# A two-layer decoder trunk on one core: modulation weights transposed in DRAM and summed along the free axis, weight units stored as SBUF holds them

## The chip, the cores and the metric

The kernel runs on one core of a Trainium2 chip. The metric is the time of one execution on the device in microseconds (us); lower is better. The engines that matter here are TensorE (PE, with its weight loads as PEld), VectorE (DVE), ScalarE (ACT), GpSimd (POOL) and SyncE (SP), whose queue issues nearly all transfers from DRAM. They run side by side, each working through its own instructions in order, and they wait for one another through semaphores.

## The reference, cut to what matters

One sequence of 256 tokens with 2048 features passes through two layers. Layer 0 mixes by causal pooling, layer 1 by multi-head latent attention; each has a SwiGLU feed-forward part (FFN) with 5632 inner features. Every sub-layer gets a shift, a scale and a gate, which are vectors of 2048 numbers computed from one conditioning vector `c`:

```python
sc = jax.nn.silu(c)                                   # (1, 2048)
for i in range(2):
    shift_m, scale_m, gate_m, shift_f, scale_f, gate_f = split(sc @ mod_w[i] + mod_b[i], 6)
    if i == 1:
        kv_shift, kv_scale = split(sc @ kv_mod_w + kv_mod_b, 2)
        h_kv = rmsnorm(x, kv_in_norm) * (1 + kv_scale) + kv_shift
        kv = shared_kv(h_kv, ...)
    h = rmsnorm(x, norm_mix[i]) * (1 + scale_m) + shift_m
    x = x + gate_m * (pool_mixer(h) if i == 0 else mla_mixer(h, kv))
    h = rmsnorm(x, norm_ffn[i]) * (1 + scale_f) + shift_f
    x = x + gate_f * ((silu(h @ ffn_gate[i]) * (h @ ffn_up[i])) @ ffn_down[i])
return rmsnorm(x, final_norm)
```

`mod_w[i]` has 2048 rows and 6 x 2048 columns. Each of these products is one row times a large matrix: 14 vectors of 2048 results from 16 MB of weights each (12 from `mod_w`, 2 from `kv_mod_w`), all float32.

## The kernel before, in words

**Weight units.** The large products run on TensorE. A weight unit is a block of 512 rows and 512 columns (1 MB). `w_unit` loads it into a slot of the ring "raw" (six slots of 8 KB per partition), ScalarE writes its upper half (L440), VectorE the rest (L442), both into the ring "hl", and TensorE multiplies with three combinations of halves: 24 matmuls of 512 columns per unit (L464). In DRAM the weights lie as in the reference, so a partition of a unit is four pieces of 2 KB.

**The opening.** The first four modulation products (shift, scale and gate of the pooling mixer, and the first 512 columns of the FFN's shift and scale) are needed at once. `Strips` computes them on TensorE with 32-column weights (L274), 16 units of 1 MB for each of the first three (rows of 8 KB), and 8 units for the last, each loaded as two transfers of 512 KB whose rows are pieces of 2 KB. Some of the gate's units are summed on VectorE instead (L257, L259). The order of work in this stage is written out by hand.

**The background.** All other modulation products run on VectorE beside the matmuls. `Part` handles one vector of 2048 results: for each of 16 row blocks of the weight (128 x 2048) one instruction adds weight times `s_col` (silu of `c`, one number per partition) to an accumulator of 128 x 2048 (L230). `BlockPart` handles 512 columns of shift and of scale together: 8 units, each loaded as two transfers and added with two instructions of 128 x 1024 (L305). The accumulator then holds 128 partial sums per column. `folded` sums them: per 512 columns one 32 x 32 block transpose (L320) and one reduction (L321) on VectorE, then a matmul with a 0/1 matrix (L326), and four small VectorE instructions on 32 partitions each, which write the columns (L343, L346, L357, L935, L936). The bias comes in by loading it into row 0 of the accumulator, which POOL sets to zero first (L220, L298).

**Pace.** `background` is a list of these units. Each weight unit calls `tick`, which issues background units at a planned rate (`plan`, `release`); `flush` runs what stands in `pending` after a given number of weight units, placed behind that unit's two halves. `folded` puts its pieces there while `pieced` is true; during the attention stage it issues them at once. The scheduler of the framework orders the rest by priority; the stretches between an FFN and what follows are in a written order.

**End of an FFN.** `FFN_STEPS` gives the order of a layer's FFN: p for a chunk of gate and up projection, t for its transposition, d for a group of the down projection. The last are "p10 t9 t10 d3". `StreamEnd` adds the gated result to the stream. Its method `known` does what doesn't need the last group: for 512 columns and both token tiles it multiplies the sum so far by the gate (L673) and adds the stream (L674). In d3 it is called for the first columns at the start and for the next columns at each step.

**Vectors.** Norm gains, `c` and the biases of the opening are loaded as rows by eight small transfers and turned on TensorE (L192, L200, L205).

Of the kernel before, what the change touches and what calls it, by code (L numbers as in the profile page):

```python
# [17 lines left out]
P = 128  # L18
# [31 lines left out]
C_FOLD = C_SIGN + 1  # L50
C_SEL = C_FOLD + P
# [14 lines left out]


LATE, MLA_LATE, WO_LATE = 3, 5, 3

FOLD_WAIT = 2  # L70

V_NM, V_NF, V_KVIN, V_KVN, V_QN, V_PS, V_END = 0, 32, 64, 80, 84, 88, 104


def shape_constants():
    con = np.zeros((P, C_END), np.float32)
    con[:, C_ID:C_ID + P] = np.eye(P, dtype=np.float32)
    q = np.arange(P)
    con[:, C_MASK:C_MASK + P] = np.where(q[None, :] <= q[:, None], 0.0, NEG)
    freq = (10000.0 ** (-np.arange(0, ROPE, 2, dtype=np.float64) / ROPE)).astype(np.float32)  # L80
    con[:, C_FREQ] = freq[q % HALF]
    con[:, C_FOLD:C_FOLD + P] = q[:, None] % 32 == q[None, :] % 32
# [13 lines left out]
def tile_trunk(ctx: ExitStack, tc: tile.TileContext, a: dict, out: bass.AP):  # L96
# [41 lines left out]
    fold = con[:, C_FOLD:C_FOLD + P]  # L138
    crow = t2k([KD, P])
    vrows = t2k([V_END, P])  # L140
    brows = t2k([5 * KD, P])
# [3 lines left out]

    def load_rows(first, name, pattern, **sizes):
        src = a[name].rearrange(pattern, q=P)
        sync.dma_start(vrows[first:first + src.shape[0]], src)
# [13 lines left out]
    load_rows(V_NM, "norm_mix", "l (r q) -> (l r) q")  # L162
    load_ahead()
    load_rows(V_NF, "norm_ffn", "l (r q) -> (l r) q")
    load_rows(V_KVIN, "kv_in_norm", "(r q) -> r q")
    load_x(1)
    load_rows(V_KVN, "kv_norm", "(r q) -> r q")
    load_ahead()
    load_rows(V_QN, "q_norm", "l (r q) -> (l r) q")
    load_rows(V_PS, "pool_scale", "l (r q) -> (l r) q")  # L170
    load_ahead()
    sync.dma_start(brows, a["mod_b"][0, :5 * D].rearrange("(r q) -> r q", q=P))
# [10 lines left out]
    front = work.tile([P, KD * (STRIP + 7) + STRIP], F32, tag="acc", bufs=2, name="front")  # L183
    s_strip = front[:, :KD * STRIP].rearrange("p (k m) -> p k m", m=STRIP)
    one_strip = front[:, KD * (STRIP + 7):]
    bcol = front[:, KD * STRIP:KD * (STRIP + 5)].rearrange("p (i k) -> p i k", k=KD)
    gm_col, ps_col = (front[:, KD * (STRIP + i):KD * (STRIP + i + 1)] for i in (5, 6))
    pool.memset(front[:, :KD * STRIP], 0.0)
    pool.memset(one_strip, 0.0)
    pool.memset(one_strip[:, 0:1], 1.0)  # L190
    cps = ps_t()
    pe.transpose(cps[:, :KD], crow, ident[:KD, :KD])  # L192
    s_col = const.tile([P, KD], F32, name="s_col")
    act.activation(s_col, cps[:, :KD], AF.Silu)
    dve.tensor_copy(s_strip[:, :, 0], s_col)
    vcol = const.tile([P, V_PS], F32, name="vcol")

    def vectors():
        vps = ps_t()
        pe.transpose(vps[:, :V_END], vrows, ident[:V_END, :V_END])  # L200
        dve.tensor_copy(vcol, vps[:, :V_PS])
        dve.tensor_copy(ps_col, vps[:, V_PS:V_END])

        bps = ps_t()
        pe.transpose(bps[:, :5 * KD], brows, ident[:5 * KD, :5 * KD])  # L205
        for i in range(5):
            dve.tensor_scalar(out=bcol[:, i], in0=bps[:, i * KD:(i + 1) * KD], scalar1=1.0 if i in (1, 4) else 0.0,
                              scalar2=None, op0=ALU.add)
# [4 lines left out]
    class Part:  # L213
        def __init__(self, w, b, done):
            self.w, self.b, self.done, self.kt = w, b, done, 0

        def unit(self):
            if self.kt == 0:
                self.acc = work.tile([P, D], F32, tag="acc", bufs=2, name=nm("acc"))
                pool.memset(self.acc, 0.0)  # L220
                sync.dma_start(self.acc[0:1, :], self.b)
            r = raw_t([P, D])
            sync.dma_start(r, self.w[self.kt * P:(self.kt + 1) * P, :])
            self.add(r)
            self.kt += 1
            if self.kt == KD:
                self.done(self.acc)

        def add(self, r):
            dve.scalar_tensor_tensor(out=self.acc, in0=r, scalar=s_col[:, self.kt:self.kt + 1],  # L230
                                     in1=self.acc, op0=ALU.mult, op1=ALU.add)
# [3 lines left out]
    class Strips:  # L235
        def __init__(self, i, pair, done, aside=()):
            self.aside, self.acc, self.bank = aside, None, None
            self.n, self.rows, self.done, self.kt = (2, 2, done, 0) if pair else (NSTRIP, 1, done, 0)
            w = a["mod_w"][0][:, i * D:(i + self.rows) * D]
            self.w = w.rearrange("(k p) (i n) -> p k i n", p=P, i=2)[:, :, :, :CH] if pair else                 w.rearrange("(k p) (i n) -> p k i n", p=P, i=NSTRIP)  # L240
# [10 lines left out]
        def use(self, r):  # L251
            last = self.kt + self.rows == KD
            if self.kt in self.aside:
                s_ = s_col[:, self.kt:self.kt + 1]
                if self.acc is None:
                    self.acc = work.tile([P, 1, NSTRIP, CH], F32, tag="acc", bufs=2, name=nm("acc"))
# [31 lines left out]


    class BlockPart:  # L290
        def __init__(self, w, b, col, done):
            self.w, self.b, self.col, self.done, self.kt = w, b, col, done, 0

        def unit(self):
            pick = slice(self.col, self.col + CH)
            if self.kt == 0:
                self.acc = work.tile([P, 2, CH], F32, tag="acc", bufs=2, name=nm("acc"))
                pool.memset(self.acc, 0.0)  # L298
                sync.dma_start(self.acc[0:1], self.b.rearrange("o (i n) -> o i n", i=2)[:, :, pick])
            r = raw_t([P, 2, 2, CH])  # L300
            rows = self.w[self.kt * P:(self.kt + 2) * P, :].rearrange("(k p) (i n) -> p k i n", p=P, i=2)
            for k in range(2):
                sync.dma_start(r[:, k], rows[:, k, :, pick])
            for k in range(2):
                dve.scalar_tensor_tensor(out=self.acc, in0=r[:, k], scalar=s_col[:, self.kt + k:self.kt + k + 1],  # L305
                                         in1=self.acc, op0=ALU.mult, op1=ALU.add)
            self.kt += 2
            if self.kt == KD:
                self.done(self.acc)

    pending, pieced = [], [True]

    def folded(acc, n, fin):


        part = acc[:, :n // 32]

        def piece(i):
            tr, ns = t2k([P, CH]), slice(i * CH, (i + 1) * CH)
            dve.transpose(tr, acc[:, ns])  # L320
            dve.tensor_reduce(out=part[:, i * (CH // 32):(i + 1) * (CH // 32)], in_=tr.rearrange("p (b j) -> p b j", j=32),  # L321
                              axis=AX.X, op=ALU.add)

        def finish():
            pt = ps_t()
            pe.matmul(pt[:, :n // 32], lhsT=fold, rhs=part, start=True, stop=True)  # L326
            v = pt[:, :n // 32].rearrange("p (k r) -> p k r", r=4)
            for r in range(4):
                rows = slice(32 * r, 32 * r + 32)
                fin(v[rows, :, r], rows)  # L330
        n_ = n // CH
        for i in range(n_):
            if pieced[0]:
                pending.append((i // 2 if n_ == 2 else i, lambda i=i: piece(i)))
            else:
                piece(i)
        pending.append((n_ + 1 if pieced[0] and n_ > 2 else FOLD_WAIT, finish))

    def to_cols_folded(fin):
        return lambda acc: folded(acc, D, fin)  # L340

    def shift_to(i):
        return to_cols_folded(lambda pt, rows: dve.tensor_copy(cols[rows, i, :], pt))  # L343

    def scale_to(i, g):
        return to_cols_folded(lambda pt, rows: dve.scalar_tensor_tensor(  # L346
            out=cols[rows, i, :], in0=pt, scalar=1.0, in1=vcol[rows, g:g + KD], op0=ALU.add, op1=ALU.mult))
# [3 lines left out]
    def gate_to(name):  # L351
# [3 lines left out]

        def fin(pt, rows):
            dve.tensor_copy(col[rows], pt)  # L357
            if rows.stop == P:
                pending.append((0, spread))
# [9 lines left out]
        return to_cols_folded(fin)  # L369

    def mod_part(l, i, done):
        cs = slice(i * D, (i + 1) * D)
        return Part(a["mod_w"][l][:, cs], a["mod_b"][l:l + 1, cs], done)

    def kv_part(i, done):
        cs = slice(i * D, (i + 1) * D)
        return Part(a["kv_mod_w"][:, cs], a["kv_mod_b"][None, cs], done)
# [70 lines left out]
    def w_unit(src):  # L448
        if repr(src) in early:
            return early.pop(repr(src))  # L450
        shape = [P, KL, src.shape[1]]
        r = raw_t(shape)
        w_load[0] = sync.dma_start(r, src.rearrange("(k p) n -> p k n", p=P))
# [23 lines left out]
    def proj(src, tiles):  # L477
        banks = [ps_t() for _ in range(NT)]
        for u in range(len(tiles)):
            hi, lo = w_unit(src[u * CH:(u + 1) * CH, :])  # L480
# [1152 lines left out]
```

## Time and profile before

| | |
|---|---|
| median of 3 runs | 1937.2 us (1936.84 to 1937.63) |
| the profiled execution | 1935.94 us, span of the trace 1934.2 us |
| TensorE granted clock, mean | 0.983 |
| busy: PE, DVE, ACT, POOL | 97%, 77%, 44%, 3% |
| moved by DMA | 575.08 MB, mean 297 GB/s |

All rows below are from that one execution. "Busy" is the time in which an engine had an instruction under way; for TensorE it includes the overlap of pipelined matmuls, so 100% busy isn't yet full speed. A row of waits names the engine and line that sat idle, what released it, and the total, the number and the longest of these waits. A row of windows gives for a stretch of the span each engine's busy time and instruction count, the granted TensorE clock, the busy share of the DMA engines and their rate. A row of groups gives a line's engine, operation, tiles, shapes and count, then total busy time and mean ns of one, then the idle time just before them.

### The profile page before, as it was taken

The numbers are of one execution on the slowest core, as the hardware profiler recorded it, in microseconds if no ns is written. First come the engines' busy times: TensorE is split into PE (matmuls) and PEld (weight loads), VectorE is DVE, ScalarE is ACT, GpSimd is POOL, SyncE is SP. The second block draws the span as 40 slices with busy tenths as digits, with TensorE's granted clock in tenths as the row PEclk, the third lists the DMA queues.
The fourth block names the chain that finished last, engine by engine and source line by source line (L and its number), as shares of the span: only waits on it lengthen the run. The fifth ranks groups of instructions, "written<-read, shape, count | busy, mean of one in ns | idle before, by whom it ended". The sixth has DMA issues, their size and how long they took to land.

```text
span 1934.2 us, 22338 instructions
## 1 busy us (share of the span) xinstructions
PE 1866.6 (97%) x8836; PEld 1511.7 (78%) x8836; DVE 1482.1 (77%) x1419; ACT 849.2 (44%) x954; POOL 49.4 (3%) x46
## 2 busy tenths in 40 slices
PE   6689999999999999999999999999999999999998
PEld 3156887888888888787879888888888888888887
DVE  2148899999878788888799986989886565555656
ACT  3024634443433344335678735634444433333333
POOL 0000000000000000001200000000000000000000
PEclk9689999999999999999999999999999999999999
DMA  9999999889898999998698695998886667666651
GB/s 397 411 416 387 386 364 320 303 308 362 322 344 318 339 336 331 353 337 273 214 341 297 213 332 187 386 334 312 279 291 239 231 240 255 235 205 236 218 196 44
DMA packets 226114, 575.08 MB, mean 297 GB/s; under 512 B 12109, under 2 KB 16709, under 8 KB 203859
## 3 DMA queue, kind: packets, MB, share of 16 engines
q1 hardware_dynamic: 225482, 570.49, 81.5%
q0 software_dynamic: 432, 3.15, 0.4%
q8 instruction: 69, 1.13, 0.2%
q14 instruction: 35, 0.29, 0.0%
q10 hardware_dynamic: 96, 0.02, 0.0%
HBM read 567.31 MB, written 6.32 MB: 297 GB/s over the span
## 4 chain that ended last, share of the span: by engine, by line
PE 89%; DMA 5%; DVE 3%; ACT 2%; issue 1%; POOL 0%; SPq 0%; POOLq 0%; DVEq 0%; ACTq 0%
PE ps L464 77%; DMA raw<-in_mod_w_dram 4%; PE ps L473 2%; PE ps L1048 2%; PE ps L1363 2%; PE ps L274 1%; PE ps L798 1%; DVE hl L442 1%; DMA act<-in_x_dram 1%; DVE acc L230 1%; PE ps L1271 1%; DMA raw<-in_ffn_up_dram 0%; PE ps L606 0%; PE ps L1023 0%; PE ps L840 0%
## 5 line engine op out<-in xcount | busy, mean ns | idle before, releaser
L464 PE MATMUL ps<-hl,act 128*128 128x512 f32 x6744 | 1549.7, 391 | 6.9 <-DVE hl L442 4.3
L464 PEld LDWEIGHTS ps<-hl,act 128*128 128x128 f32 x6744 | 1266.2, 188 | 271.5 <-DVE hl L442 5.2
L440 ACT ACTIVATE hl<-raw 128x2048 fp32r<-128x2048 f32 x289 | 552.9, 1917 | 619.9 <-PE ps L464 505.4
L442 DVE TENSOR_TENSOR hl<-raw,hl 128x2048 fp32r<-128x2048 f32 x289 | 660.7, 2288 | 201.4 <-ACT hl L440 200.6
L230 DVE SCALAR_TENSOR_TENSOR acc<-raw,s_col,acc 128x2048 f32<-128x2048 f32 x112 | 262.8, 2346 | 0.7 <-DMA raw<-in_mod_w_dram 0.6
L305 DVE SCALAR_TENSOR_TENSOR acc<-raw,s_col,acc 128x1024 f32<-128x1024 f32 x112 | 143.4, 1280 | 2.2 <-DMA raw<-in_mod_w_dram 0.7
L274 PE MATMUL ps<-raw,front 128*32 128x512 f32 x392 | 66.6, 744 | 25.6 <-DMA raw<-in_mod_w_dram 25.5
L767 DVE TENSOR_TENSOR act<-ps,act 128x512 f32<-128x512 f32 x96 | 64.1, 684 | 10.5 <-PE ps L464 10.2
L274 PEld LDWEIGHTS ps<-raw,front 128*32 128x32 f32 x392 | 9.7, 119 | 60.9 <-DMA raw<-in_mod_w_dram 48.4
L1363 PE MATMUL ps<-act,hl 128*128 128x256 f32 x384 | 48.8, 284 | 0.0
L473 PE MATMUL ps<-hl,act 128*128 128x512 f32 x192 | 47.0, 399 | 1.2 <-DVE act L569 0.9
L1363 PEld LDWEIGHTS ps<-act,hl 128*128 128x128 f32 x384 | 47.5, 192 | 0.7 <-DVE act L1327 0.2
L801 ACT ACTIVATE act<-ps 128x512 fp32r<-128x512 f32 x44 | 23.8, 595 | 52.6 <-PE ps L798 45.0
L281 DVE COPY t2k<-ps 128x256 f32<-128x256 f32 x4 | 1.7, 424 | 57.5 <-ACT t2k L280 57.5
L856 DVE TENSOR_TENSOR x<-ps,x 128x512 f32<-128x512 f32 x32 | 22.1, 691 | 30.1 <-PE ps L464 30.1
L473 PEld LDWEIGHTS ps<-hl,act 128*128 128x128 f32 x192 | 35.1, 188 | 10.9 <-ACT act L556 1.8
L867 ACT ACTIVATE t2k<-ps 128x512 f32<-128x512 f32 x24 | 14.2, 592 | 62.6 <-PE ps L464 62.5
L493 ACT ACTIVATE junk<-x 128x512 bf16<-128x512 f32 x23 | 14.6, 633 | 60.7 <-DVE x L681 39.9
L871 DVE TENSOR_TENSOR t2k<-ps,t2k 128x512 f32<-128x512 f32 x24 | 16.5, 688 | 25.3 <-PE ps L464 25.3
L1048 PEld LDWEIGHTS ps<-act,act 128*128 128x128 f32 x128 | 24.5, 198 | 11.5 <-issue 8.4
L1048 PE MATMUL ps<-act,act 128*128 128x256 f32 x128 | 31.7, 400 | 0.0
L802 DVE TENSOR_TENSOR act<-ps,act 128x512 fp32r<-128x512 f32 x44 | 28.2, 684 | 4.3 <-ACT act L801 4.1
(233 smaller groups left out, 1001.6 us busy)
## 6 DMA issues: line engine op xcount, KB each, us to landing
raw<-in_mod_w_dram SPq DMA_DIRECT2D x128, 1024.0 KB, 6.9
raw<-in_ffn_gate_dram SPq DMA_DIRECT2D x88, 1024.0 KB, 5.7
raw<-in_ffn_up_dram SPq DMA_DIRECT2D x88, 1024.0 KB, 6.5
raw<-in_ffn_down_dram SPq DMA_DIRECT2D x88, 1024.0 KB, 5.5
raw<-in_mod_w_dram SPq DMA_DIRECT2D x128, 512.0 KB, 6.5
raw<-in_kv_mod_w_dram SPq DMA_DIRECT2D x32, 1024.0 KB, 5.9
raw<-in_w_o_dram SPq DMA_DIRECT2D x16, 1024.0 KB, 8.8
raw<-in_w_uq_dram SPq DMA_DIRECT2D x8, 768.0 KB, 5.1
```

The lines of the kernel that those rows point to most:

```text
L230: dve.scalar_tensor_tensor(out=self.acc, in0=r, scalar=s_col[:, self.kt:self.kt + 1], in1=self.acc, op0=ALU.mult, op1=ALU.add)
L274: pe.matmul(self.bank[m * STRIP:(m + 1) * STRIP, :], lhsT=weights(k), rhs=r[:, k, i, :], start=first, stop=last)
L305: dve.scalar_tensor_tensor(out=self.acc, in0=r[:, k], scalar=s_col[:, self.kt + k:self.kt + k + 1], in1=self.acc, op0=ALU.mult, op1=ALU.add)
L440: hi_ins = act.activation(hi, r, AF.Copy)
L442: lo_ins = dve.tensor_tensor(out=lo, in0=r, in1=hi.bitcast(F32), op=ALU.subtract)
L464: pe.matmul(banks[tok], lhsT=t_[:, i, k, tok * P:(tok + 1) * P], rhs=w[:, k, :], start=first and n < len(part), stop=last and n >= len(ord ...
L473: pe.matmul(bank, lhsT=t_[:, i, k, tok * P:(tok + 1) * P], rhs=w[:, k, :], start=first and n == 0, stop=last and n == len(order) - 1)
L767: dve.tensor_tensor(out=part, in0=banks[tok], in1=part, op=ALU.add)
L801: act.activation(m[:, 0, :, ts_], v, AF.Copy)
L802: dve.tensor_tensor(out=m[:, 1, :, ts_], in0=v, in1=m[:, 0, :, ts_].bitcast(F32), op=ALU.subtract)
L1048: pe.matmul(mixed[g][:, n % 2, :], lhsT=wp[g][:, k, ns], rhs=pool_all[g // 2][:, g % 2, k, :], start=k == 0, stop=k == KL - 1)
L1363: pe.matmul(pt[:, h, :], lhsT=w(h0 + h, k), rhs=t_[:, i, k, :], start=n == 0, stop=n == 3 * KL - 1)
```

## The change

- `mod_w` and `kv_mod_w` are also laid out transposed in DRAM, on the host. A background unit is now 128 results by 2048 inputs, one transfer of 1 MB whose rows are 8 KB. One VectorE instruction multiplies it with `s_row` (silu of `c`, the same on all partitions) and sums along the free axis into one column of `sums`; the product goes back into the raw tile. `BlockPart` is gone: its work is a `Part` of 8 such units.
- `folded`, its transposes, reductions and matmuls, the accumulators, their memsets and bias loads are gone. The results already are columns; one or two small VectorE instructions add bias and apply the gain.
- All weights of w_unit, and the opening's last product, are laid out so that a unit is one contiguous megabyte, 8 KB per partition.
- Vectors are stored as columns and loaded by one transfer (128 x 344) ahead of `x`. A second copy of `c`, as a row, is spread over the partitions by four matmuls with a row of ones (`silu_row`).
- `known` is cut into 8 pieces (columns by token tile) that go to `pending` at chunk p10, with the waits in `KNOWN`; the flush at the start of d3 is gone.

```diff
+KNOWN = (1, 3, 5, 7, 9, 10, 11, 12)
-FOLD_WAIT = 2
...
+    sync.dma_start(vcol, a["vectors"])
     load_x(0)
-    sync.dma_start(crow, a["c"].rearrange("b (r q) -> (b r) q", q=P))
     sync.dma_start(con, a["con"])
...
+    def silu_row():
+        act.activation(crow, crow, AF.Silu)
+        for j in range(ND):
+            js = slice(j * CH, (j + 1) * CH)
+            pt = ps_t()
+            pe.matmul(pt, lhsT=ones[0:1, :], rhs=crow[:, js], start=True, stop=True)
+            act.activation(s_row[:, js], pt, AF.Copy)
...
     class Part:
         def unit(self):
-            if self.kt == 0:
-                self.acc = work.tile([P, D], F32, tag="acc", bufs=2, name=nm("acc"))
-                pool.memset(self.acc, 0.0)
-                sync.dma_start(self.acc[0:1, :], self.b)
+            if self.n == 0:
+                self.sums = work.tile([P, KD], F32, tag="sums", bufs=3, name=nm("sums"))
             r = raw_t([P, D])
-            sync.dma_start(r, self.w[self.kt * P:(self.kt + 1) * P, :])
-            self.add(r)
-        def add(self, r):
-            dve.scalar_tensor_tensor(out=self.acc, in0=r, scalar=s_col[:, self.kt:self.kt + 1],
-                                     in1=self.acc, op0=ALU.mult, op1=ALU.add)
+            sync.dma_start(r, self.w[self.tiles[self.n] * P:(self.tiles[self.n] + 1) * P, :])
+            dve.scalar_tensor_tensor(out=r, in0=r, scalar=1.0, in1=s_row, op0=ALU.mult, op1=ALU.mult,
+                                     accum_out=self.sums[:, self.n:self.n + 1])
...
         def load(self):                      # Strips
             r = raw_t([P, self.rows, self.n, CH])
-            for k in range(self.rows):
-                sync.dma_start(r[:, k], self.w[:, self.kt + k])
+            sync.dma_start(r.rearrange("p k i n -> p (k i n)"), self.w[self.kt // self.rows])
...
-    class BlockPart:
-    def folded(acc, n, fin):
...
+    def shift_to(i, first):
+        return lambda sums: dve.tensor_tensor(out=cols[:, i, :], in0=sums, in1=bias(first, KD), op=ALU.add)
+    def scaled_sums(dst, sums, first, g):
+        dve.scalar_tensor_tensor(out=dst, in0=sums, scalar=1.0, in1=bias(first, dst.shape[1]), op0=ALU.add, op1=ALU.add)
+        dve.tensor_tensor(out=dst, in0=dst, in1=vcol[:, g:g + dst.shape[1]], op=ALU.mult)
...
     def w_unit(src):
-        w_load[0] = sync.dma_start(r, src.rearrange("(k p) n -> p k n", p=P))
+        w_load[0] = sync.dma_start(r.rearrange("p k n -> p (k n)"), src)
...
-            self.known(0)
-        def known(self, j):
+        def known(self, j, tok, gate):
...
-                flush()
                 end = stream_end[0]
                 end.start(gates[gate_name])
...
-                    if last and c == g[0]:
-                        end.known(j + 1)
...
             if c == NF - 1:
-                stream_end.append(StreamEnd(l))
+                end = StreamEnd(l)
+                stream_end.append(end)
+                for n, wait in enumerate(KNOWN):
+                    pending.append((wait, lambda n=n: end.known(n // NT, n % NT, gates[gate_name])))
...
+def units(w):
+    k, n = w.shape
+    w = w.reshape(k // CH, KL, P, n // CH, CH).transpose(0, 3, 2, 1, 4)
+    return w.reshape(k // CH, n // CH, P, KL * CH)
...
+    o["mod_wt"] = o["mod_w"].transpose(0, 2, 1)
+    o["kv_mod_wt"] = np.asarray(i["kv_mod_w"]).T
+    block = o["mod_w"][0].reshape(KD // 2, 2, P, 6, D)[:, :, :, 3:5, :CH]
+    o["mod_block"] = block.transpose(0, 2, 1, 3, 4).reshape(KD // 2, P, 4 * CH)
```

More of the change, by code (lines that the diff above doesn't have):

```diff
@@ L311, in tile_trunk @@
-    pending, pieced = [], [True]
-    def folded(acc, n, fin):
[L316 to L347, printed above, removed]
+    pending = []
+    def shift_to(i, first):
+        return lambda sums: dve.tensor_tensor(out=cols[:, i, :], in0=sums, in1=bias(first, KD), op=ALU.add)
```

213 lines of the change are left out of this document (88 added, 125 removed).

## The prediction

> **What bounds the kernel now.** I read the page first, then the chain of work that ended last, then TensorE's waits after the opening, then windows by stage.
>
> ```profile
> span 1934.2 us, 22338 instructions
> ...
> PE 1866.6 (97%) x8836; PEld 1511.7 (78%) x8836; DVE 1482.1 (77%) x1419; ACT 849.2 (44%) x954; POOL 49.4 (3%) x46
> ```
>
> TensorE is busy for 97% of the span, so what the change does to VectorE counts only where TensorE waits for it. The chain shows two parts.
>
> ```profile
> 169.52 56.22 PE ps L464 x240
> 225.88 62.49 PE ps L464 x276
> ```
>
> Until 169.5 us the opening runs; from there the chain is matmuls back to back, 62.49 / 276 = 226 ns each. How the opening is bound is seen in two windows of it (the last two columns are DMA busy share and GB/s):
>
> ```profile
> 145.00:165.00 20.00, 19.09 (x121) 9.94 (x122) 16.07 (x34) 10.64 (x18) 1.22 (x2) 1.00 1.05 387
> 20.00:140.00 120.00, 96.63 (x540) 46.24 (x536) 41.00 (x86) 21.11 (x42) 0.00 (x0) 0.82 1.02 416
> ```
>
> The DMA engines are full in both, so the opening lasts as long as its bytes. The rate differs: 416 GB/s while nearly all loads have rows of 8 KB, 387 where the last product and the first weight units come in pieces of 2 KB. For the rest, TensorE's waits from 169 us to the end:
>
> ```profile
> PE ps L464 <- DVE hl L442: 4.3, 1, 4.3
> PE ps L326 <- issue: 4.3, 1, 4.3
> PE ps L1483 <- ACT t2k L1476: 3.1, 2, 1.6
> PE ps L464 <- DVE cols L936: 1.2, 2, 0.8
> ...
> PE ps L326 <- DVE act L767: 0.5, 1, 0.5
> ...
> PE ps L464 <- DVE act L767: 0.3, 1, 0.3
> ```
>
> These are 13.7 us of waits in 1764.7 us. So the ceiling is low whatever VectorE saves: these waits, the fold's own matmuls, and the slow end of the opening.
>
> **The change part by part.** *Contiguous weight units and the opening.* In the window 145 to 165 the bytes at 416 instead of 387 GB/s take 20 x 387 / 416 = 18.6 us: 1.4 us less. The slow rate starts a little before the window; I take 1.5. Bounds: 0, if the slower rate has another cause than the pieces, and 2.1, if all of the last 29.5 us before 169.5 us shorten by that ratio. Small loads: 8 row loads (100 KB) and 64 KB of `con` go, 172 KB of columns and 8 KB of row `c` come; 16 KB more at 416 GB/s are 0.04 us, taken as nothing. The columns stand ahead of `x`, which delays it by 172 KB, 0.4 us; the stage's total of bytes hides it. The three vector turns on TensorE and `silu_row` (four matmuls, one activation over 2048 columns on one partition) fall into this stage, where TensorE is 80% busy at 20 to 140 us by the row above and waits for DMA: nothing. Without that cover `silu_row`'s four matmuls of 512 columns would cost at least 4 x 226 ns, 0.9 us.
>
> [...]
>
> After the opening no wait on a load stands among TensorE's waits above, so faster weight loads there are worth nothing. SP also issues less (one transfer for two in 56 + 8 units, no bias loads); nothing waits for it.
>
> *The new instruction.* Before, these groups:
>
> ```profile
> L230 DVE SCALAR_TENSOR_TENSOR acc<-raw,s_col,acc 128x2048 f32<-128x2048 f32 x112 | 262.8, 2346 | 0.7 <-DMA raw<-in_mod_w_dram 0.6
> L305 DVE SCALAR_TENSOR_TENSOR acc<-raw,s_col,acc 128x1024 f32<-128x1024 f32 x112 | 143.4, 1280 | 2.2 <-DMA raw<-in_mod_w_dram 0.7
> ...
> L320 DVE STREAM_TRANSPOSE t2k<-acc 128x512 f32<-128x512 f32 x42 | 28.8, 698 | 0.1
> L321 DVE TENSOR_REDUCE acc<-t2k 128x16 f32<-128x512 f32 x42 | 27.9, 678 | 0.6
> ...
> L1470 DVE TENSOR_TENSOR sm<-sm 128x1 f32<-128x1 f32 x16 | 2.4, 151 | 0.0
> ```
>
> An accumulator output on VectorE doesn't appear in this trace. Below it lies L230, the same operation with two fp32 tensors in SBUF: 2346 ns. Above it lies a second pass of a reduction, 4 x 678 = 2712 ns more. It could be under L230 by little at most, since the same 2048 elements of two tensors are read; I exclude a gain. I take 2346 plus one 128x1 instruction of 151 ns, 2.50 us, because it is nearest in form: a multiply and a sum in one instruction. VectorE then spends 168 x 2.50 = 420 us where it spent 262.8 + 143.4 + 28.8 + 27.9 = 463 us, some 43 us less, and the small finishing instructions drop from 4 or 8 per fold to 1 to 3. That is off the path but for the waits below. If an accumulating instruction lands just ahead of one that TensorE waits for, it costs 0.15 us.
>
> *The fold.* Its matmuls are on TensorE's own queue:
>
> ```profile
> L326 PE MATMUL ps<-acc,con x28: 191/274/297, 225.6 to 1747.0; 128*128 128x32 f32 x14, 128*128 128x64 f32 x14
> ```
>
> and the longest wait is at one of them. TensorE's and then VectorE's instructions in order of time:
>
> ```profile
> 975.85 1.03 PE L606 MATMUL ps<-con,t2k 128*128 128x128 f32 x8
> 981.14 0.41 PE L326 MATMUL ps<-acc,con 128*128 128x64 f32 x2 [4.26 <-issue]
> 981.36 7.32 PE L464 MATMUL ps<-hl,act 128*128 128x512 f32 x24
> ```
> ```profile
> 974.02 2.28 DVE L442 TENSOR_TENSOR hl<-raw,hl 128x2048 fp32r<-128x2048 f32 x1
> 976.22 1.29 DVE L320 STREAM_TRANSPOSE t2k<-acc 128x512 f32<-128x512 f32 x2
> 977.44 1.23 DVE L321 TENSOR_REDUCE acc<-t2k 128x16 f32<-128x512 f32 x2
> ...
> 979.81 1.23 DVE L321 TENSOR_REDUCE acc<-t2k 128x16 f32<-128x512 f32 x2
> 980.97 2.27 DVE L442 TENSOR_TENSOR hl<-raw,hl 128x2048 fp32r<-128x2048 f32 x1
> ```
>
> TensorE stands at the fold's matmul from 976.9 to 981.1 us while VectorE transposes and reduces, although the halves for the next 24 matmuls were ready at 976.3. Without the fold these matmuls start at once and the next L442 moves up 4.8 us. What is late next is ScalarE's modulation, which needs the finished columns; two small instructions behind the last sum give them. I take all 4.3 us; bounds 2, if that modulation delays the turns after the 24 matmuls, and 4.3. The matmuls themselves: the pair at 981.14 holds the next one until 981.36, 0.22 us; 14 pairs are 3.1 us (bounds 2 and 3.1, since some sit within a wait). The three small rows of the wait list (1.2, 0.5 and 0.3 us) are waits at fold matmuls or behind VectorE's eight small instructions for a block: 2.0 us, bounds 0 and 2.0.
>
> *`known`.* The other wait of 4.3 us:
>
> ```profile
> 812.66 1.28 DVE L674 TENSOR_TENSOR act<-x,act 128x512 f32<-128x512 f32 x2
> 814.54 0.69 DVE L856 TENSOR_TENSOR x<-ps,x 128x512 f32<-128x512 f32 x1 [0.60 <-PE ps L464]
> ...
> 816.35 2.49 DVE L674 TENSOR_TENSOR act<-x,act 128x512 f32<-128x512 f32 x4
> ...
> 820.09 4.48 DVE L442 TENSOR_TENSOR hl<-raw,hl 128x2048 fp32r<-128x2048 f32 x2
> ```
> ```profile
> 822.43 9.74 PE L464 MATMUL ps<-hl,act 128*128 128x512 f32 x30 [4.30 <-DVE hl L442]
> ```
>
> The pieces of `known` run in a heap from 815 to 820 us, ahead of the half that TensorE needs. The change deals them out over 12 weight units, behind each unit's halves, and makes pieces half as long (two instructions, 1.4 us). I take 4.3; bounds 0, if they heap up at another place, and 4.3. The work is moved, not added. The first two sit behind the first units of p10, so they need the gate earlier than before; the gate's vector is finished long before, since its background is spread over the FFN's first units.
>
> *Attention.* ScalarE's softmax keeps TensorE waiting for 3.1 us in two places, and VectorE feeds ScalarE there. VectorE is rid of 1.4 us per 512 columns of fold in that stage but gets 22 accumulator reads. I take half, 1.5 us; bounds 3.1 and minus 3.3 (22 x 0.15, all on the path).
>
> Sum: 1.5 + 4.3 + 3.1 + 2.0 + 4.3 + 1.5 = 16.7 us. The profiled execution took 1935.94 us, with 1.7 us around its span; it becomes 1919.2. The median of the runs lies 1.3 us higher: 1920.5 us. At their lower ends the terms give 0 + 2 + 2 + 0 + 0 - 3.3 = 0.7, at their upper ends 18.9.
>
> **The rivals.** *The sum costs a second pass.* If multiplying and summing don't run together, each unit takes 2346 + 2712 = 5058 ns. VectorE's load by stage, and the units in it (only the named line's time in the last four rows):
>
> ```profile
> 169.50:900.00 730.50, 724.90 (x3224) 599.19 (x3225) 650.92 (x514) 300.65 (x241) 13.49 (x10) 0.99 0.93 338
> 900.00:1097.00 197.00, 187.20 (x1160) 165.90 (x1158) 177.46 (x261) 148.36 (x303) 23.61 (x13) 0.99 0.73 259
> 1097.00:1316.00 219.00, 218.16 (x978) 179.12 (x976) 186.29 (x190) 107.60 (x128) 6.40 (x7) 1.00 0.87 307
> ```
> ```profile
> 169.50:900.00 730.50, 173.60 (x74) 0.99 0.93 338
> 900.00:1097.00 197.00, 51.62 (x22) 0.99 0.73 259
> ```
> ```profile
> 169.50:900.00 730.50, 61.45 (x48) 0.99 0.93 338
> 1097.00:1316.00 219.00, 61.49 (x48) 1.00 0.87 307
> ```
>
> In the first stage 74 units grow by 2.71 us and 24 (48 halves at 1.28) by 2.50: 650.9 + 260.5 = 911 us in 730.5, 181 over. In the second 177.5 + 59.7 = 237, 40 over; in the third 186.3 + 60 = 246, 27 over. Less at most the 56.7 us of all transposes and reductions, the kernel loses 191 us and comes to some 2125 us. It decides once a unit grows by more than the slack: (730.5 - 650.9) / 98 = 0.8 us. For it speaks that a transposing and a reducing instruction were used before at 678 to 698 ns per 512; against it that L230 already takes two fp32 tensors at 1.15 ns per element. Chance 0.09.
>
> [...]
>
> *The waits come back elsewhere.* VectorE is 89% busy (650.9 of 730.5) up to 900 us. If a dealt-out piece of `known` or the last sum of a vector still lands ahead of a needed half, the two terms of 4.3 keep only 1.5 together and attention gives nothing: 1.5 + 3.1 + 2.0 + 1.5 = 8.1, so 1929 us. Against it: no load is added to that stretch. Chance 0.17.
>
> *Nothing reaches the end.* TensorE starts 4 us earlier behind each wait but meets the next late load: DMA is 93% busy up to 900 us. Then only some 2 us stay: 1935 us. Against it: rows of 8 KB raise the rate by 7%. Chance 0.05.
>
> *More.* Attention runs with VectorE 90% busy (177.5 of 197) and loses more idle time and slow joins than I counted: 1912 us. Chance 0.04.
>
> **How the numbers follow.** The forecast has the remaining 0.65. Its own range is 1915 to 1930, from most terms at their upper ends to two of them failing. The range reaches to the second and the last rival: 1911 to 1933. Measurement tells 0.2%, 3.9 us, from no change. Faster by that: 0.65 + 0.17 + 0.04, less a little of the first, 0.84; the same: 0.05; slower: the first rival and unforeseen order, 0.11.
>
> **What the profile after would show.** The summing group at 2.4 to 2.6 us for 168 instructions; no transposes and no fold matmuls; 415 GB/s up to the opening's end, and the first L464 near 168 us; no wait of TensorE above 2 us around 800 to 830 and around 970 to 985 us. Wrong would be: a unit above 3.1 us; or waits of L464 on L442 with L673, L674 or the summing line ahead of it.

## The result, and the profile after

The changed kernel takes 1917.9 us (median of 4 runs, 1917.6 to 1920.0) against 1937.1 us; the ratio is 0.9903, 95% interval 0.9886 to 0.9920. 1920.5 us was forecast, with a range of 1911 to 1933. The profiled execution took 1918.19 us.

The page after, the two lines shown of before:

```profile
span 1916.4 us, 21930 instructions
...
PE 1862.8 (97%) x8813; PEld 1507.8 (79%) x8813; DVE 1402.7 (73%) x1391; ACT 850.2 (44%) x958; POOL 26.9 (1%) x32
```

VectorE lost 79 us of work, the span 18. The span is read stage by stage, between the first starts of lines that both kernels have (L464, L798, L473, L1271, L1363 and L1459 of before; L398, L729, L407, L1197, L1288 and L1383 of after; from each line's first or last start in its trace; us):

| stage | before | after | gain |
|---|---|---|---|
| opening, to the first large matmul | 169.5 | 169.4 | 0.1 |
| to the first transposition of the first FFN | 222.0 | 219.4 | 2.6 |
| to the handover at that FFN's end | 508.5 | 500.0 | 8.5 |
| handover, to the first product of the key latent | 27.8 | 30.0 | -2.2 |
| to the first head product | 19.2 | 19.1 | 0.1 |
| keys, values, queries, to the first scores | 87.3 | 80.9 | 6.4 |
| from the first to the last scores | 61.5 | 62.1 | -0.6 |
| to the end of the second handover | 105.6 | 105.1 | 0.5 |
| second FFN and end | 732.8 | 730.4 | 2.4 |

A total near the forecast hides an opening that gave nothing in this execution, and a handover and scores that took longer. TensorE's waits after the opening:

```profile
PE ps L1407 <- ACT t2k L1400: 2.2, 2, 2.0
PE ps L482 <- DVE t2k L476: 1.4, 1, 1.4
PE ps L407 <- DVE act L503: 1.2, 1, 1.2
PE ps L398 <- DVE hl L376: 1.0, 2, 0.6
...
```

Both waits of 4.3 us and those at folds are gone. New is 1.4 us at L482, in the handover. (L376 is L442 of before, L482 is L548.)

### The profile page after: what moved, and what is told of

Read it like the earlier page. It is cut to its first block, busy times and chain, and to the rows that moved or that the text cites. A ratio compares the mean times of both kernels' runs of the same rounds, so it can differ in the third digit from the quotient of the medians.

```text
span 1916.4 us, 21930 instructions
## 1 busy us (share of the span) xinstructions
PE 1862.8 (97%) x8813; PEld 1507.8 (79%) x8813; DVE 1402.7 (73%) x1391; ACT 850.2 (44%) x958; POOL 26.9 (1%) x32
## 4 chain that ended last, share of the span: by engine, by line
PE 69%; issue 22%; DMA 3%; DVE 3%; ACT 1%; SPq 0%; POOL 0%; POOLq 0%; DVEq 0%; ACTq 0%
PE ps L398 58%; DMA raw<-in_mod_w_dram 3%; PE ps L256 2%; PE ps L973 2%; PE ps L407 2%; PE ps L1288 2%; DVE raw L211 1%; PE ps L729 1%; PE ps L1197 1%; PE ps L540 0%; DMA raw<-in_mod_block_dram 0%; PE ps L196 0%; PE ps L948 0%; PE ps L770 0%; DVE hl L376 0%
## 5 line engine op out<-in xcount | busy, mean ns | idle before, releaser
L398 PE MATMUL ps<-hl,act 128*128 128x512 f32 x6744 | 1539.5, 390 | 1.9 <-DVE hl L376 1.0
L398 PEld LDWEIGHTS ps<-hl,act 128*128 128x128 f32 x6744 | 1263.0, 188 | 264.7 <-DVE hl L376 1.8
L376 DVE TENSOR_TENSOR hl<-raw,hl 128x2048 fp32r<-128x2048 f32 x289 | 661.1, 2289 | 253.2 <-ACT hl L374 252.5
L211 DVE SCALAR_TENSOR_TENSOR raw<-raw,s_row 128x2048 f32<-128x2048 f32 x168 | 383.2, 2284 | 3.6 <-DMA raw<-in_mod_wt_dram 3.6
L256 PE MATMUL ps<-raw,s_strip 128*32 128x512 f32 x392 | 65.2, 760 | 34.6 <-DMA raw<-in_mod_w_dram 33.5
L256 PEld LDWEIGHTS ps<-raw,s_strip 128*32 128x32 f32 x392 | 9.5, 121 | 70.0 <-DMA raw<-in_mod_w_dram 46.3
L1288 PE MATMUL ps<-act,hl 128*128 128x256 f32 x384 | 49.6, 287 | 0.0
L1288 PEld LDWEIGHTS ps<-act,hl 128*128 128x128 f32 x384 | 48.3, 195 | 0.7 <-DVE act L1253 0.2
L407 PE MATMUL ps<-hl,act 128*128 128x512 f32 x192 | 47.0, 400 | 1.2 <-DVE act L503 1.2
L407 PEld LDWEIGHTS ps<-hl,act 128*128 128x128 f32 x192 | 35.2, 188 | 10.7 <-ACT act L490 2.3
L798 ACT ACTIVATE t2k<-ps 128x512 f32<-128x512 f32 x24 | 14.2, 590 | 47.9 <-PE ps L398 47.9
L696 ACT ACTIVATE act<-ps 128x512 f32<-128x512 f32 x32 | 19.1, 597 | 29.0 <-PE ps L398 28.8
## 6 DMA issues: line engine op xcount, KB each, us to landing
raw<-in_mod_w_dram SPq DMA_DIRECT2D x48, 1024.0 KB, 12.1
```

Source lines behind the costliest of these rows:

```text
L211: dve.scalar_tensor_tensor(out=r, in0=r, scalar=1.0, in1=s_row, op0=ALU.mult, op1=ALU.mult, accum_out=self.sums[:, self.n:self.n + 1])
L256: pe.matmul(self.bank[m * STRIP:(m + 1) * STRIP, :], lhsT=weights(k), rhs=r[:, k, i, :], start=first, stop=last)
L376: lo_ins = dve.tensor_tensor(out=lo, in0=r, in1=hi.bitcast(F32), op=ALU.subtract)
L398: pe.matmul(banks[tok], lhsT=t_[:, i, k, tok * P:(tok + 1) * P], rhs=w[:, k, :], start=first and n < len(part), stop=last and n >= len(ord ...
L407: pe.matmul(bank, lhsT=t_[:, i, k, tok * P:(tok + 1) * P], rhs=w[:, k, :], start=first and n == 0, stop=last and n == len(order) - 1)
L1288: pe.matmul(pt[:, h, :], lhsT=w(h0 + h, k), rhs=t_[:, i, k, :], start=n == 0, stop=n == 3 * KL - 1)
```

## The experiments

The runs went in three groups of four, each beside the kernel before: the first (`silu_row` later, `known` undone, pieces, the sum alone) and the third (the changed kernel again and the last three) on one chip, the second (dealing out alone, the two prices of a unit, the hold) on another; the medians of before were 1935.8, 1935.8 and 1935.0 us. The runs of one kernel spread over 0.8 to 4.8 us, so single terms are read from the stages of the traces, one trace for each kernel. Stages that an edit doesn't touch mostly repeat to 0.2 us. Three don't: the opening (168.2 to 170.8 us where it is the same program), the stage behind it and the scores. What they vary with is shown below, at the spread matmuls, under attention and in the last section. The changed kernel itself, run again:

> The changed kernel itself, unedited, on the same chip as the next three, to compare with: 0.990 of the kernel before.

It took 1917.6 us, ratio 0.9906 (0.9891 to 0.9921): the forecast of this run held.

**Dealing out `known`, undone.** The edit puts the old calls back:

```diff
-                for n, wait in enumerate(KNOWN):
-                    pending.append((wait, lambda n=n: end.known(n // NT, n % NT, gates[gate_name])))
+                flush()                                   # at the start of d3, as before
+            for tok in range(NT):                         # in StreamEnd.start, and for j + 1 at each step of d3
+                self.known(0, tok, gate)
```

> The changed kernel, with StreamEnd.known as before the change (called at the start of d3 and at each of its steps, with the flush ahead of it). Theory A: dealing it out was worth the 4.3 us wait at 818 us less the 2.2 us that the handover lost (a background unit now lands ahead of the gated piece): undoing it costs about 2 us, 1920, and the wait of L398 on L376 of about 4 us is back while the handover's 2.2 us go. Rival B: the wait went because VectorE has less to do without folds: no wait over 1 us comes back, 1918 or less.

1923.3 us, ratio 0.9935 (0.9923 to 0.9948). The first row of TensorE's waits after the opening in this run:

```profile
PE ps L398 <- DVE hl L376: 4.3, 1, 4.3
```

The wait is back to the tenth although VectorE has no folds, so rival B falls. By stages the first FFN up to the handover takes 505.7 us instead of 500.0, the handover 27.9 instead of 30.0. Dealing out is worth 5.7 us and costs 2.1 in the handover, 3.6 together, more than theory A's 2. The spans of the traces differ by 2.7 us (1919.1 against 1916.4), mainly because the scores, which the edit doesn't touch, took 1.5 us less here, and the medians by 5.7.

**Dealing out alone, in the kernel before.**

> The kernel before, with only the dealing out of known (8 pieces at the waits 1, 3, 5, 7, 9, 10, 11, 12 from chunk p10, no flush at d3). Theory A: the wait of 4.3 us of L464 on L442 at 818 us goes, and some of it is lost in the handover: 1933 to 1935. Rival B: with the folds still there the pieces heap up again or push others: 1937 or more.

1932.8 us, ratio 0.9986 (0.9977 to 0.9995), an interval that lies wholly below 1, and a little less than theory A's 1933 to 1935. Stages: 502.4 us instead of 508.5 up to the handover, 30.2 instead of 27.8 in it, and none after. TensorE's waits now begin with the fold:

```profile
PE ps L327 <- issue: 4.3, 1, 4.3
```

So the two waits of 4.3 us are independent: each goes with its own part of the change. (The next run is the other half of this: the fold's wait is gone there and the one at L442 is back, there L402 on L380, 4.3 us.)

**The sum without folds, alone** (both other parts undone).

> The changed kernel with both of the former undone: known as before the change and weight units in pieces of 2 KB. What is left is the transposed modulation weights with the sum in one instruction, no folds, and vectors as columns. Theory A: the sum without folds alone gives the fold's wait (4.3), its matmuls (3.1), the small waits (2.0) and about 2 us in attention: 11 to 13 us less than before, 1924 to 1926, and the parts add up: the losses of the two other edits sum to its loss against the changed kernel within 1 us. Rival B: the parts cover for one another (one freed wait hides another): its loss is under half of that sum or above twice.

1923.7 us, ratio 0.9940 (0.9927 to 0.9952): 12.1 us less than before, as theory A said. Against the kernel before its stages gain 2.6, 2.1, 0.0, 0.1, 6.4, 0.9, 0.5 and 2.4 us (from the second row of the table on), 15.0 together; the opening loses 2.7. That the parts add up within 1 us isn't confirmed: by medians, against the changed kernel at 1917.6, undoing `known` costs 5.7 us, the pieces 1.9 and both 6.1; by spans of the traces 2.7, 0.3 and 5.5. By neither is the loss under half of the sum of the two or above twice, so rival B isn't shown either.

**Pieces of 2 KB.** A unit stays one contiguous megabyte, but a partition's 8 KB are four pieces:

```diff
-        w_load[0] = sync.dma_start(r.rearrange("p k n -> p (k n)"), src)
+        w_load[0] = sync.dma_start(r, src.rearrange("k p n -> p k n"))
-    w = w.reshape(k // CH, KL, P, n // CH, CH).transpose(0, 3, 2, 1, 4)
+    w = w.reshape(k // CH, KL, P, n // CH, CH).transpose(0, 3, 1, 2, 4)
```

> The changed kernel, with each weight unit and each unit of the opening's last product still one contiguous megabyte in DRAM but ordered so that a partition's 8 KB are four pieces of 2 KB. Theory A: the pieces alone make the rate 387 instead of 419 GB/s at 145 to 165 us; the opening ends about 1.8 us later and the rest of the kernel doesn't change, 1919.7. Rival B: the strided rows of the old layout made the lower rate, not the pieces: the rate stays at 419, 1918. Rival C: the lower DMA load also helps after the opening: more than 4 us slower.

The window 145 to 165 us of the changed kernel, and then of this one (last columns DMA share and GB/s):

```profile
145.00:165.00 20.00, 18.56 (x137) 9.88 (x130) 15.19 (x33) 11.07 (x20) 0.70 (x1) 1.00 1.01 419
```
```profile
145.00:165.00 20.00, 16.71 (x122) 9.02 (x118) 15.20 (x32) 10.79 (x18) 0.70 (x1) 1.00 1.05 387
```

387 GB/s is the number of the kernel before: it is the piece, not the stride of the rows in DRAM (rival B falls). The first large matmul comes 1.7 us later, at 171.1 us. The opening itself scatters, but the rate doesn't: it is 386 or 387 GB/s in this window in all four traces with pieces and 418 to 420 in the ten others, and the two kernels with pieces and `silu_row` (171.1 and, in the run before, 172.2 us) start later than the seven that differ from them here in the rows alone (168.2 to 170.8). Up to the first scores the two kernels then stay 1.7 to 1.8 us apart, so faster loads are worth nothing after the opening (rival C falls); the stage of scores takes 60.7 us instead of 62.1, which hides most of it at the end. 1919.6 us, ratio 0.9920 (0.9907 to 0.9934).

**`silu_row` later.**

> The changed kernel, with the four matmuls that spread silu(c) (silu_row) issued after unit 19 of the opening instead of unit 3. Theory A: they hold TensorE for 7.2 us at 21 to 28 us while it has work, the ring of loads falls behind, and the DMA engines drop to 333 and 388 GB/s at 55 to 65 us, which ate the gain of the larger rows. Then the rate stays near 415 GB/s up to 65 us, the first large matmul comes 1.4 to 2 us earlier (167.4 to 168 instead of 169.4 us) and the whole takes about 1916.3 us. Rival B: the opening is bound by its bytes anyway and the dip is made up: no change, 1917.9 within 0.7.

1917.6 us, ratio 0.9908 (0.9894 to 0.9921): no gain beyond the spread, as rival B said. But its reason isn't the one at work. The matmuls kept together for 7.2 us at 66 us did there what they had done at 21 us: 28.54 MB came between 30 and 100 us, against 28.96 before and 28.32 in the changed kernel. The first large matmul came 0.8 us earlier, at 168.6 us, half of theory A's gain, and the next stage gave it back (220.3 us instead of 219.4; the last section has the reason). Spread out they do better, in the last run but one.

**The price of a unit: 0.69 us more, and 2.37 us more.**

```diff
                                      accum_out=self.sums[:, self.n:self.n + 1])
+            dve.tensor_tensor(out=r[:, :CH], in0=r[:, :CH], in1=s_row[:, :CH], op=ALU.mult)        # one run
+            dve.scalar_tensor_tensor(out=r, in0=r, scalar=1.0, in1=s_row, op0=ALU.mult, op1=ALU.mult,
+                                     accum_out=self.sums[:, KD + self.n:KD + self.n + 1])           # the other
```

> The changed kernel with one more VectorE instruction of 512 columns (about 0.69 us) behind each of the 168 sums, 116 us in all; its product isn't used. Theory A: the slack of VectorE up to 900 us is over 0.8 us per unit on average, and now more, so the steady stretches don't slow down; only stretches where VectorE is nearly full (attention, the handover) lose, 3 to 8 us: 1921 to 1926. Rival B: averages deceive, VectorE is on the path wherever a unit lands ahead of a half: a large part of the 116 us shows, over 30 us slower.

> The changed kernel with each of the 168 summing instructions issued twice (the second into columns that aren't used), 2.37 us more per unit, about 398 us of VectorE in all: the price that the prediction's slower rival put on a second pass. Theory A: VectorE becomes the bound in the stretches with background: by the prediction's working with 2.37 in place of 2.71 us and the folds already gone, from 1918 to some 2060 to 2110 us. Rival B: the schedule absorbs it up to the next stage, under 2000 us.

0.69 us per unit, 115 us in all, costs 11 us: 1928.7 us, ratio 0.9964 (0.9950 to 0.9978), more than the 3 to 8 expected and far from rival B. Three windows of it: the first FFN to the handover, the handover, and keys to scores.

```profile
392.00:891.80 499.80, 499.80 (x2250) 414.59 (x2249) 453.19 (x398) 198.49 (x148) 0.70 (x1) 1.00 0.87 337
891.80:925.20 33.40, 27.93 (x122) 21.33 (x121) 27.29 (x38) 17.56 (x37) 17.76 (x8) 0.95 0.58 201
944.30:1029.10 84.80, 81.22 (x499) 72.03 (x497) 83.10 (x99) 61.27 (x100) 3.33 (x2) 1.00 0.90 341
```

The FFN takes the same 499.8 us with VectorE 41 us fuller; the handover loses 3.4 us and the stage to the scores 3.9. The stage ahead of the FFN, up to its first transposition, takes 222.0 us where the changed kernel took 219.4 and 220.6 in its two traces. Twice the instruction takes 2088.9 us (ratio 1.0788, 1.0772 to 1.0804), inside theory A's range. Here VectorE is the bound:

```profile
169.80:900.00 730.20, 678.37 (x2911) 549.61 (x2912) 721.60 (x621) 272.97 (x212) 1.23 (x2) 0.96 0.80 303
```

721.6 of 730.2 us. So the forecast's slower rival was priced about rightly in the total: 171 us for 2.37 us per unit, where the rival had some 190 for 2.71. Its threshold of 0.8 us per unit is only bracketed: at 0.69 the first FFN isn't slower and the stage ahead of it by 1.4 to 2.6 us, at 2.37 both are, by 68 and 34 us. It was not narrowed further.

**The background held earlier at the handover.** `hold()` moves from the last step of d3 to the last but one.

> The changed kernel, with the background held one step earlier at the end of the first FFN (from the last step but one of the down projection's last group). The units that don't run there run later. Theory A: the handover loses 2.2 us because a summing instruction (2.37 us) sits on VectorE at 894 us ahead of the gated piece that the norm waits for; without it the handover is 2 us shorter and the total about 1916, if the unit finds room later. Rival B: the handover is bound by something else, or the units run later in attention where VectorE is full: no gain or up to 3 us slower.

VectorE in order of time, in the changed kernel and with the hold:

```profile
894.28 2.29 DVE L211 SCALAR_TENSOR_TENSOR raw<-raw,s_row 128x2048 f32<-128x2048 f32 x1
...
896.75 0.68 DVE L611 TENSOR_TENSOR x<-ps,gate 128x512 f32<-128x512 f32 x1
```
```profile
895.72 0.69 DVE L611 TENSOR_TENSOR x<-ps,gate 128x512 f32<-128x512 f32 x1 [1.54 <-PE ps L407]
```

In the changed kernel the gated piece L611, on which the norm and all that follows depend, stands behind a background unit; with the hold it waits for TensorE alone. The handover takes 27.5 us instead of 30.0. Yet the total is 1919.0 us, ratio 0.9912 (0.9897 to 0.9927): 16 units instead of 14 now run in the stage from keys to scores, which takes 83.1 us instead of 80.9. Theory A's cause is right and its total wrong; rival B's second half came true.

**A place for the held units; the matmuls spread; more background early.**

```diff
-FFN0_UNITS = 95 ... LATE, MLA_LATE, WO_LATE = 3, 5, 3
+FFN0_UNITS = 91 ... LATE, MLA_LATE, WO_LATE = 3, 0, 3      # last run: -6
+    for j in range(ND):                                    # last two runs
+        then(19 + 2 * j, silu_spread, j)                   # one matmul of silu_row each
```

> The changed kernel with the background held one step earlier at the end of the first FFN (as in the run that gained 2.5 us in the handover and lost 2.2 us in attention), and with the five background units that ran between that FFN and the heads now paced into the first FFN (MLA_LATE 0, 91 units). Theory A: attention gave the time back because VectorE is 96% busy there (77.26 of 80.9 us) and the held unit landed in it; in the first FFN VectorE has 87 us of slack (412.5 busy of 499.8), so the handover's 2.4 us stay and attention isn't slower: 2.5 to 3.5 us faster than the changed kernel. Rival B: attention takes its 143 us whatever VectorE does, as TensorE's own work there is nearly as long, and what is gained ahead of it is lost: within 1 us of the changed kernel.

1920.3 us, ratio 0.9921 (0.9907 to 0.9936). Keys to scores stay at 81.1 us and the handover at 27.6, as theory A said, but the first FFN, with 76 units instead of 69, now takes 503.6 us instead of 500.0, though VectorE has idle time there on average. 2.3 us of TensorE's waits stand in it now, on halves of ScalarE (1.4 us) and VectorE, against 0.2 us; the other 1.5 us weren't traced. Nothing was won.

> The former with the four matmuls of silu_row issued one at a time after units 19, 21, 23 and 25 of the opening instead of together after unit 3. Theory A: 7.2 us of TensorE in one piece makes the ring of loads fall behind wherever it stands (at unit 3 it cost 0.64 MB by 100 us, at unit 19 0.42 MB); pieces of 1.8 us fit between units that wait for loads. The DMA rate from 20 to 100 us then is as before the change (28.9 MB between 30 and 100 us), and the first large matmul comes at about 167.7 us: 1.5 us faster than the former run. Rival B: the lost bytes come from elsewhere, no change.

1918.5 us, ratio 0.9912 (0.9897 to 0.9927). Theory A's sign is there: 28.89 MB come between 30 and 100 us and the first large matmul at 168.3 us, against 27.89 MB and 170.8 us in the run before it. The windows at 55 to 65 us of before, of the changed kernel and of this one:

```profile
55.00:65.00 10.00, 6.78 (x48) 1.87 (x48) 7.50 (x22) 0.96 (x3) 0.00 (x0) 0.92 1.01 419
```
```profile
55.00:65.00 10.00, 9.45 (x84) 4.27 (x76) 4.06 (x13) 1.83 (x4) 0.00 (x0) 1.00 0.94 360
```
```profile
55.00:65.00 10.00, 7.97 (x62) 2.44 (x54) 7.07 (x21) 0.38 (x1) 0.00 (x0) 0.95 1.01 418
```

The dip stood in eight of the nine traces with `silu_row` at unit 3 (354 to 373 GB/s); in the ninth, the changed kernel run again, the rate was 421 and the opening ended at 168.2 us. The same four matmuls, in the changed kernel and in the ninth trace:

```profile
20.93 7.19 PE L196 MATMUL ps<-act,ones 1*128 1x512 f32 x8
```
```profile
20.86 3.92 PE L196 MATMUL ps<-act,ones 1*128 1x512 f32 x8
```

In all eight traces with the dip they took 7.19 us in one piece (1056 ns for the median instruction), in the one without it 3.92 us (587 ns). So the dip goes with slow matmuls, and what varies from run to run is how long they take. The granted clock reads 0.50 around them in three of the traces with 1056 ns (the sum alone, the price of 0.69 us, and the run before this one), but 1.00 in the five others, so it was not shown that half the clock is the reason. Spread out, the eight instructions took 587 to 1217 ns, and neither trace has the dip; with one in nine traces free of it without spreading, two traces say little of how much the spreading itself did.

> The former with six more background units moved from the heads' stage of attention into the first FFN (MLA_LATE -6). Theory A: attention is bound by VectorE and softmax together, 6 x 2.37 = 14 us less VectorE work there gives 1 to 3 us. Rival B: TensorE's own work binds attention once the handover's unit is out of it: no gain, and with VectorE fuller in the first FFN up to 2 us slower.

1917.4 us, ratio 0.9907 (0.9891 to 0.9924), no different from the changed kernel. Keys to scores take 80.5 us with VectorE busy for 65.1 us there instead of 71.8, and TensorE is busy in all 80.5, so its own work bounds that stage: rival B. No version tried beats the changed kernel beyond the spread.

## Why the prediction was right, step by step

*The opening: wrong in one step, the total saved by others.* The rate of 387 against 416 GB/s was read rightly, and larger rows are worth 1.7 us between the two traces (1.5 forecast). But the sign that the forecast gave for them, the first large matmul near 168 us, failed: it came at 169.4. The step that failed is "this stage ... waits for DMA: nothing" for `silu_row`, which had at least 0.9 us as its price without cover. It cost 7.2 us of TensorE in one piece in the changed kernel's trace, 3.9 us at best (the four matmuls are eight instructions in the rows of L196 above), four to eight times that price, and from there TensorE has a backlog until about 65 us. TensorE frees the six slots of the ring here, and SyncE's longest wait for it to do so between 20 and 32 us went from 5.0 us before (on L274) to 8.5 (on L256); so the loads fell behind and up to 1.1 MB less came between 30 and 100 us (27.89 against 28.96). In the one trace of the changed kernel with 3.9 us the first large matmul came at 168.2 us, near the forecast. A busy share of 80% over 120 us was the wrong view for it: the cover was looked up for the stage and not for the place.

*The new instruction.* 2.50 us were forecast:

```profile
L211 DVE SCALAR_TENSOR_TENSOR raw<-raw,s_row 128x2048 f32<-128x2048 f32 x168 | 383.2, 2284 | 3.6 <-DMA raw<-in_mod_wt_dram 3.6
...
L211 DVE DVE_READ_ACCUMULATOR raw<-raw,s_row 128x1 f32 x168 | 13.9, 83 | 0.0
```

2.37 us: the instruction is 62 ns faster than L230, a gain that the forecast excluded, and the read of the accumulator takes 83 ns, not 151. Whether the gain comes from the constant that stands as its scalar in place of a column was not shown; no run changed that alone. With the sum the instruction takes 1.12 ns per element (2284 / 2048), no slower than L230 without one: 1.15 (2346 / 2048).

*The fold.* The mechanism was right, the size too small: with attention 4.3 + 2.0 + 3.1 + 1.5 = 10.9 us were forecast, and the sum alone gains 15.0 us after the opening. Of the excess, 2.1 us lie in keys to scores (6.4, where 4.3 was the wait). The step that failed there is the price of a wait as its length alone: behind this one TensorE ran slowly. The kernel before, in the four us behind it (the granted clock is the third number from the right):

```profile
981.00:985.00 4.00, 3.86 (x11) 3.16 (x12) 3.93 (x7) 1.09 (x3) 0.95 (x1) 0.58 0.86 279
```

The forecast's own row of L464 at 981.36 has it: 24 matmuls in 7.32 us, where 24 at 226 ns are 5.4, so 1.9 us more. Over the whole stage TensorE's idle time fell by 4.6 us and the busy time of the same 192 matmuls of that line from 47.2 to 45.5 us. Another 2.6 us lie in the FFNs and the second handover (2.6 + 2.1 + 0.1 + 0.5 + 2.4, where 5.1 stood for matmuls and small waits). Which joins gave these wasn't tried.

*`known`.* 4.3 forecast; 5.7 up to the handover, less 2.1 in it. The 5.7 exceed the 4.3 for the same reason as the fold: in the kernel before, the granted clock was 0.50 from 822.4 to 826 us, right behind the wait. The loss in the handover is akin to the forecast's second rival, a piece or sum that still lands ahead of something needed; it was a summing unit ahead of the gated piece, and it cost 2.1 us where the rival had 8.6. So the total near the forecast is in part luck: what the opening and the handover missed, the slow matmuls behind the two waits brought in.

*Attention.* 1.5 us were forecast between 0 and 3.1 for the softmax waits. They went from 3.1 to 2.2 us; the stage of scores gained nothing in the changed kernel's traces, and took 62.1 us against 61.5; with the clock kept it took 60.6 to 60.7, 0.8 to 0.9 less than before. Why it is 62.1 in the changed kernel and 60.7 with pieces shows in the granted clock from 1032 to 1040 us (the third number from the right), first in the changed kernel and then with pieces:

```profile
1032.00:1040.00 8.00, 8.00 (x52) 7.79 (x51) 7.12 (x13) 5.79 (x20) 0.00 (x0) 0.80 0.92 344
```
```profile
1032.00:1040.00 8.00, 7.45 (x57) 7.24 (x58) 7.77 (x20) 7.22 (x21) 0.00 (x0) 1.00 0.77 269
```

Both have the same wait for ScalarE shortly before; TensorE in order of time, in the changed kernel and with pieces:

```profile
1030.81 0.55 PE L1407 MATMUL ps<-con,t2k 128*128 128x128 f32 x3 [1.97 <-ACT t2k L1400]
```
```profile
1032.55 0.55 PE L1411 MATMUL ps<-con,t2k 128*128 128x128 f32 x3 [1.97 <-ACT t2k L1404]
```

Only in the first does the clock fall after it, and matmuls of 256 columns go from 0.12 to 0.21 us each. Six traces agree: the changed kernel, its second run and `silu_row` later have 0.58 to 0.67 in the four us behind this wait and 62.1 or 62.2 us for the scores; pieces, `known` undone and the sum alone have 1.00 and 60.6 or 60.7. The last section has the other place.

## What to carry to other kernels

Cover for an added piece of work is to be looked up at its place and on its engine, not as a busy share of its stage: four small matmuls, priced at 0.9 us and taking 3.9 to 7.2, ate the gain of a better layout in eight of nine traces. In a kernel bound by one engine at 97%, list that engine's waits and price each part of a change by the waits it removes, not by the freed time of another engine: 79 us less work on VectorE went with 18 us less span, and some of these came from the other parts. Look at the granted clock behind a long wait too: here it was 0.50 to 0.61 behind waits of 4.3 us, and the matmuls there took 1.9 to 3.0 us more. A unit of background work that is moved out of one stage appears in the next; test a move by the times of all stages, since the total alone (1917.4 to 1920.3 us for five versions here) can't show what was won and what was given back.

## What the runs showed of the hardware that was not expected

The granted clock can fall or not after the same waits, in the same kernel. At the end of the opening TensorE has three short waits in both traces of the changed kernel, 0.40 or 0.42 us for a load and 0.56 and 0.95 us for ScalarE; from 169 to 175 us the changed kernel and the same kernel run again show

```profile
169.00:175.00 6.00, 5.61 (x24) 4.27 (x25) 5.49 (x11) 3.62 (x5) 0.00 (x0) 1.00 1.00 412
```
```profile
169.00:175.00 6.00, 6.00 (x16) 4.66 (x16) 5.90 (x11) 2.78 (x4) 0.00 (x0) 0.55 1.02 418
```

24 matmuls at full clock and 16 at 0.55. The second execution began them 1.2 us earlier and both reached the first transposition at 388.8 us: the gain of an earlier start was spent on the clock. It shows in other traces as well. Of the ten traces of the changed kernel and of variants that leave this stage's work as it is, the five with 0.50 to 0.58 in this window took 220.3 to 220.6 us from the first large matmul to the first transposition, the five with 0.72 to 1.00 took 219.4 or 219.5. Equal pauses went with unequal clocks here, and behind the wait of 1.97 us in the scores too (0.80 and 1.00 from 1032 to 1040 us). What decides it was not shown: no run moved a pause on purpose.

Behind the long waits it fell each time. The traces have five waits of 4.3 us (two in the kernel before, one each with `known` undone, with dealing out alone and with the sum alone). Each was followed by a granted clock of 0.50 to 0.61 over some 4 us, and the matmuls behind it took 1.9 to 3.0 us more than at 226 ns each.
